# Gated DeltaNet in a two-layer hybrid block: k and q projected first, v only after the first batch's inverse has been written

## The chip, the cores and the metric

The kernel runs on one core of one Trainium2 chip. The metric is the time of one execution in microseconds (us), as the device reports it. The core's engines are TensorE (PE in the profile, its weight loads PEld), VectorE (DVE), ScalarE (ACT), GpSimd (POOL) and SyncE (SP), which here only issues DMA transfers.

## What is computed

The reference runs two layers over 256 context tokens and 512 latent tokens of width 1024. In each layer the tokens are normalised and modulated, multiplied by one input projection `w_in`, and its columns are shared out among four mixers: a bidirectional gated DeltaNet (GDN), a windowed attention (SWA), a spatial gating MLP and a bidirectional mLSTM. Their outputs are joined, projected and added to the stream; an MLP follows. The change is in the GDN alone, whose start is:

```python
def branch(q, k, v, a, b):
    qkv = jax.nn.silu(dwconv_centred(jnp.concatenate([q, k, v], axis=-1), conv_w))
    q, k, v = jnp.split(qkv, 3, axis=-1)
    ...
    seq = (l2norm(heads(q, GDN_HEADS)), l2norm(heads(k, GDN_HEADS)), heads(v, GDN_HEADS))
    return seq, (g, beta)
```

and whose scan, in chunks of 64 tokens, is:

```python
a = jnp.where(strict, jnp.einsum('nbhik,nbhjk->nbhij', kbeta, k) * decay, 0.0)
rhs = jnp.concatenate([v * beta[..., None], kbeta * jnp.exp(gcum)[..., None]], axis=-1)
sol = lax.linalg.triangular_solve(a + jnp.eye(GDN_CHUNK, dtype=jnp.float32), rhs,
                                  left_side=True, lower=True)
```

The decays come from the gates a and b and from no projection of q, k or v. The matrix `a` needs k, the attention needs q and k, and v stands in the right side only.

## The kernel before, in words

**Dense products.** The fp32 products are made of three half-exact ones: ScalarE rounds a weight tile into `whi` (two halves of K, L184), VectorE makes the rest `wlo` (L187), and the activations have been split likewise into `hhi` and `hlo`. The function `gemm` makes one block of 128 output columns of all 768 tokens with 48 matmuls named `mm`: 24 of 256 columns (context) and 24 of 512 columns (latent). `gemm_tok` makes token-major ones named `mmt`. A pool, `wset`, says which buffers the halves go into; each `wload` takes the next entry.

**GDN projections.** A loop of six blocks runs in the order k0, v0, k1, v1, q0, q1 (each of k, q and v is 256 columns, two blocks). Each block is a gemm; then ScalarE copies the result into `raw` and starts a five-tap convolution, VectorE adds four taps (one SCALAR_TENSOR_TENSOR of 128x770 each, L190), and a SiLU follows: three ScalarE passes with a VectorE TENSOR_SCALAR (L288) and a VectorE product. The blocks of k and q then go through `unit_rows`: a square, a matmul `l` that sums it by head, logarithm and exponential on ScalarE, and a last product on VectorE. Tiles `kq` hold k and q by block, tiles `vf` hold v. In layer 1 q is projected for the latent tokens alone.

**Gates.** Behind the loop, small matmuls `gc` and `glps` and short VectorE steps (`gtmp`, `kds`) make the cumulative decays.

**GDN batches.** The 12 chunks of 64 tokens are worked in six batches of two chunks for each direction. For a batch, `gdn_pre` makes the decay matrix (matmuls `rows` and `Eps`, VectorE `rhl`, `Le`, `Re`, ScalarE `E`), the products `gq` of k with k and q, and the matrix `N` (VectorE), with fp16 copies `Nh` and `Nl`; `gdn_inv` inverts in five passes, each of them matmuls `t`, VectorE `T`, matmuls `yt`, VectorE `Y`, and a VectorE transpose `Z` (the first transpose of a batch is L860, those of the passes L875), then `zt` and `nw`; `gdn_kt` makes `egps`, `kt`, and transposes v and k with `vkT`; `gdn_scan` carries the state (`rps`, `yps`, `sps`, `ops`). The driver writes: pre, inverse and kt of the first batch, pre and inverse of the second, and then the scans with pre, inverse and kt of later batches between them.

**What sets the order.** A scheduler orders the whole layer: it takes the program's order as priority and puts an instruction on its engine's list where its own estimate has it ready. Each engine then runs its list in order. So dense gemms that are written later (`sk`, `sq` and `sv` of the attention, the blocks of the spatial MLP and the mLSTM) stand among the steps of the GDN's inverse and scan.

Of the kernel before, what the change touches and what calls it, by code (L numbers as in the profile page):

```python
# [9 lines left out]
F32 = mybir.dt.float32  # L10
# [14 lines left out]
EPS = 1e-6  # L25
NEG = -1e30
GAP = NT + 2
P1 = [1, 0, 5, 4, 3, 2]
MIXK = (4, 5, 0, 1, 6, 7, 2, 3)
ALL = ((0, 256), (256, 512))  # L30
# [4 lines left out]
C_GQ, C_GK, C_GV, C_GZ, C_AB = 0, 256, 512, 768, 1024  # L35
# [107 lines left out]
def flow_kernel(ctx, tc, t, out, dbg=None, stop=None):  # L143
# [9 lines left out]
    wsp = ctx.enter_context(tc.tile_pool(name="wsp", bufs=2))  # L153
# [311 lines left out]
    wset = []  # L465
# [29 lines left out]
    def gemm(parts, acts, segs, n=128, order=None, pb=None, w2=None):  # L495

        w2 = w2 or wload(parts, order)
        outs = {bank(c0): (pb or ps)("mm") for c0, cn in segs}
        for hf, (whi, wlo) in enumerate(w2):
            for c0, cn in segs:  # L500
                o = outs[bank(c0)]
                for k in range(4):
                    ahi, alo = acts[4 * hf + k]
                    for pi, (w, a) in enumerate(((whi, ahi), (whi, alo), (wlo, ahi))):
                        mm(o[0:n, 0:cn], w[:, k, 0:n], a[:, c0:c0 + cn],
                           start=(hf == 0 and k == 0 and pi == 0), stop=(hf == 1 and k == 3 and pi == 2))
        return outs
# [92 lines left out]
    for l in range(DEPTH):  # L600
# [16 lines left out]
        gd = pa.enter_context(tc.tile_pool(name="gd", bufs=1))  # L617
# [6 lines left out]
        h = modulated(l, 0, ALL, nrm, tp)  # L624
# [4 lines left out]

        def temp(tag, w=GAP + 4):  # L630
            return tp.tile([128, GAP + 4], F32, tag=tag, name=tag, bufs=1 if tag == "tc" else 2)


        zg = temp("ta")
        o, o_k0 = gemm_pair(ahead, h, ALL, (32, 128))
        evac(zg[0:32], o, ALL, 32)
        o = ps("gatesT")
# [44 lines left out]
            else:  # L682
                stt(x[:, a0:], x[:, a0:], f, e[:, a0:], MUL, MUL)

        cols = [(C_GK, C_GQ, C_GV)[which] + 128 * j for which, j in ((0, 0), (2, 0), (0, 1), (2, 1), (1, 0), (1, 1))]
        ready = {}
        for i, (which, j) in enumerate(((0, 0), (2, 0), (0, 1), (2, 1), (1, 0), (1, 1))):
            qlat = which == 1 and last
            segs = LAT if qlat else ALL
            o = gemm(None, h, segs, w2=ready.pop(i)) if i else o_k0  # L690
            if i < 5:
                ready[i + 1] = wload([win[:, cols[i + 1]:cols[i + 1] + 128]])
            raw = temp("ta")
            G.memset(raw[:, 0:2], 0.0)
            G.memset(raw[:, 258:260], 0.0)
            G.memset(raw[:, 772:774], 0.0)
            if not qlat:
                act_(raw[:, 2:258], o[0][:, 0:256], AF.Copy)
            act_(raw[:, 260:772], o[1], AF.Copy)
            a0 = 258 if qlat else 0  # L700
            acc = vf[j] if which == 2 else kq[j][:, which]
            cw = R_CONV + {0: 2, 1: 0, 2: 4}[which] + j
            act_(acc[:, a0:], raw[:, a0:GAP], AF.Copy, scale=prm[l][:, cw:cw + 1])
            for tp_ in range(1, 5):
                stt(acc[:, a0:], raw[:, a0 + tp_:GAP + tp_], prm[l][:, cw + 6 * tp_:cw + 6 * tp_ + 1], acc[:, a0:], MUL, ADD)
            e = temp("tb")[:, 0:GAP] if i % 2 else gd.tile([128, 1024], F32, tag="at", name="e", bufs=2)[:, 0:GAP]
            sigmoid_(acc[:, a0:], e[:, a0:])
            tt(acc[:, a0:], acc[:, a0:], e[:, a0:], MUL)
            if len(unit) > 2 - 1:
                unit_rows()  # L710
            if which < 2:
                act_(e[:, a0:], acc[:, a0:], AF.Square)
                unit.append((acc, e, a0, 0.125 if which else None))
        while unit:
            unit_rows()

# [11 lines left out]
        o = ps("gc")  # L728
# [22 lines left out]
        for f in range(2):  # L751
            o = ps("glps")
# [4 lines left out]
                act_(glq[hp, :, :, f, :], o[hp, q:48:2].rearrange("p (s t h) -> p s t h", s=6, t=2), AF.Exp)  # L757


        wset[:] = [(wsp, "whi", "wlo")]  # L760
        mix = [None] * 8
        O = [xm.tile([128, NT], F32, tag="xm", name="O") for _ in range(2)]
        for x in O:
# [235 lines left out]

        gdn_pre(0)  # L1000
        gdn_inv(0)
        gdn_kt(0)
        gdn_pre(1)
        gdn_inv(1)
# [26 lines left out]
        o = gemm([win[:, C_SK:C_SK + 128]], h, ALL)  # L1031
        evac(sk, o, ALL)
        for g in range(2):
            mix[2 + g] = xm.tile([128, NT], F32, tag="xm", name="sq")
            o = gemm([win[:, C_SQ + 64 * g:C_SQ + 64 * g + 64], win[:, C_SQ + 128 + 64 * g:C_SQ + 192 + 64 * g]], h, osegs)
# [5 lines left out]
        o = gemm([win[:, C_SV:C_SV + 128]], h, ALL)  # L1041
# [11 lines left out]
        o = ps("wsT")  # L1053
# [19 lines left out]
        for p0, pn in ((0, 4), (4, 2)):  # L1073
            o = ps("svT")
# [15 lines left out]
        for j in range(2):  # L1090
            mix[4 + j] = xm.tile([128, NT], F32, tag="xm", name="uu")
            if early:
                o = gemm([win[:, C_MU + 128 * j:C_MU + 128 * j + 128]], h, osegs)
# [7 lines left out]
        for j in range(2):  # L1101
            mix[6 + j] = xm.tile([128, NT], F32, tag="xm", name="lq")
            for dst, base, sg2 in ((lk[j], C_LK, ALL), (mix[6 + j], C_LQ, osegs)):
                o = gemm([win[:, base + 128 * j:base + 128 * j + 128]], h, sg2)
# [4 lines left out]
        for j in range(2):  # L1109
            for p0 in range(opairs[0], NP, 4):  # L1110
                pn = min(4, NP - p0)
                o = ps("sg")
# [15 lines left out]
        o = gi("mb")  # L1128
# [17 lines left out]
        for p0, pn in ((0, 4), (4, 2)):  # L1146
            o = go1("aRp")
# [3 lines left out]
        o = gi("blp")  # L1151
# [50 lines left out]
        o = gi("Mt")  # L1202
# [4 lines left out]
        o = go1("Ml")  # L1207
# [344 lines left out]
        for n in range(8):  # L1552
            o = gemm([t["w_out"][l][:, 128 * n:128 * n + 128]], mh, osegs, order=MIXK, w2=w_next.pop() if w_next else None)
# [7 lines left out]
        w2 = [wload([t["mlp_w1"][l][:, 128 * f:128 * f + 128]]) for f in range(2)]  # L1561
# [3 lines left out]
        for fb in range(4):  # L1565
            hid = []
            for f in range(8):
                if fb == 0 and f < 2:
                    o = first[f]
                else:  # L1570
                    o = gemm([t["mlp_w1"][l][:, 1024 * fb + 128 * f:1024 * fb + 128 * f + 128]], h2, osegs)
# [65 lines left out]
```

## Time and profile before

| | |
|---|---|
| time, median of 3 runs | 1955.21 us (1955.19 to 1955.52) |
| the profiled execution | 1955.14 us, of which 1953.4 us span from the first to the last instruction |
| TensorE busy | 1874.8 us (96%), its weight loads 1536.4 us (79%) |
| VectorE busy | 1201.8 us (62%) |
| ScalarE busy | 757.4 us (39%) |
| mean granted TensorE clock | 0.977 of full speed |

The GDN of layer 0 lies at about 66 to 322 us of the span, that of layer 1 at about 1170 to 1405 us. Busy time of an engine is a sum over stages with different limits, so the stages are read apart, by windows; and a busy TensorE is not one at its peak, since the ends of matmuls are modelled.

### The profile page before, as it was taken

The numbers are of one execution on the slowest core, as the hardware profiler recorded it, in microseconds if no ns is written. First come the engines' busy times: TensorE is split into PE (matmuls) and PEld (weight loads), VectorE is DVE, ScalarE is ACT, GpSimd is POOL, SyncE is SP. The second block draws the span as 40 slices with busy tenths as digits, with TensorE's granted clock in tenths as the row PEclk, the third lists the DMA queues.
The fourth block names the chain that finished last, engine by engine and source line by source line (L and its number), as shares of the span: only waits on it lengthen the run. The fifth ranks groups of instructions, "written<-read, shape, count | busy, mean of one in ns | idle before, by whom it ended". The sixth has DMA issues, their size and how long they took to land.

```text
span 1953.4 us, 34015 instructions
## 1 busy us (share of the span) xinstructions
PE 1874.8 (96%) x14131; PEld 1536.4 (79%) x14131; DVE 1201.8 (62%) x2221; ACT 757.4 (39%) x1530; POOL 104.6 (5%) x169
## 2 busy tenths in 40 slices
PE   5999999999899999999999999999999999999998
PEld 3877778778777888888888878677777778888887
DVE  3978885666769557435535349798676754444443
ACT  4652343555524312313213236434255543333242
POOL 0021110000000000000000000211100000000001
PEclk8999999999799999999999999999999999999999
DMA  8321001121464345335433222210011323333332
GB/s 310 97 52 34 13 24 34 57 65 34 147 199 129 107 131 148 116 93 151 140 87 108 78 58 55 63 35 24 23 44 33 102 81 98 97 97 97 97 97 76
DMA packets 225955, 172.56 MB, mean 88 GB/s; under 512 B 19106, under 2 KB 208008, under 8 KB 225800
## 3 DMA queue, kind: packets, MB, share of 16 engines
q1 hardware_dynamic: 219424, 153.71, 26.6%
q10 hardware_dynamic: 4680, 10.64, 1.5%
q0 software_dynamic: 1696, 6.03, 0.9%
q8 instruction: 111, 1.82, 0.4%
q14 instruction: 44, 0.36, 0.1%
HBM read 163.02 MB, written 7.34 MB: 87 GB/s over the span
## 4 chain that ended last, share of the span: by engine, by line
PE 82%; DVE 9%; ACT 3%; DMA 3%; issue 1%; POOL 1%; DVEq 0%; ACTq 0%; SPq 0%; POOLq 0%
PE mm L181 64%; PE mmt L181 3%; PE num L181 1%; PE ops L181 1%; DMA wst<-w_in 1%; PE pv L181 1%; DVE wlo L187 1%; DVE Y L187 1%; PE adaps L181 1%; PE yt L181 1%; DVE kq L190 1%; PE t L181 1%; PE pT L1353 1%; DMA adw<-ada_w 1%; PE yps L181 1%
## 5 line engine op out<-in xcount | busy, mean ns | idle before, releaser
L184 ACT ACTIVATE whi<-wst 128x512 fp32r<-128x512 f32 (+1 forms) x388 | 241.9, 627 | 683.8 <-PE mm L181 628.8
L181 PE MATMUL mm<-hhi,whi 128*128 128x512 f32 (+3 forms) x1344 | 479.5, 362 | 11.7 <-ACT hhi L184 11.0
L181 PE MATMUL mm<-hlo,whi 128*128 128x512 f32 (+3 forms) x1344 | 479.3, 357 | 1.2 <-DVE hlo L190 1.1
L181 PE MATMUL mm<-hhi,wlo 128*128 128x512 f32 (+3 forms) x1344 | 476.3, 356 | 0.0
L187 DVE TENSOR_TENSOR wlo<-wst,whi 128x512 fp32r<-128x512 f32 (+1 forms) x388 | 265.7, 689 | 312.9 <-ACT whi L184 308.5
L181 PEld LDWEIGHTS mm<-hhi,whi 128*128 128x128 f32 (+1 forms) x1344 | 252.7, 189 | 55.2 <-ACT hhi L184 14.4
L181 PEld LDWEIGHTS mm<-hlo,whi 128*128 128x128 f32 (+1 forms) x1344 | 253.9, 189 | 38.0 <-DVE hlo L190 2.3
L181 PEld LDWEIGHTS mm<-hhi,wlo 128*128 128x128 f32 (+1 forms) x1344 | 253.2, 189 | 38.6 <-issue 1.5
L181 PE MATMUL mm<-fhi,whi 128*128 128x512 f32 (+1 forms) x784 | 275.9, 352 | 0.0
L181 PE MATMUL mm<-flo,whi 128*128 128x512 f32 (+1 forms) x784 | 275.8, 352 | 0.0
L181 PE MATMUL mm<-fhi,wlo 128*128 128x512 f32 (+1 forms) x784 | 274.5, 350 | 0.0
L190 DVE SCALAR_TENSOR_TENSOR x<-mm,mod,x 128x256 f32<-128x256 f32 (+1 forms) x122 | 79.6, 653 | 139.8 <-PE mm L181 139.7
L181 PEld LDWEIGHTS mm<-fhi,whi 128*128 128x128 f32 x784 | 148.3, 189 | 21.9 <-ACT r L184 0.8
L181 PEld LDWEIGHTS mm<-fhi,wlo 128*128 128x128 f32 x784 | 148.1, 189 | 19.7
L181 PEld LDWEIGHTS mm<-flo,whi 128*128 128x128 f32 x784 | 148.4, 189 | 19.1
L190 DVE SCALAR_TENSOR_TENSOR adacc<-adw,scT,adacc 128x1024 f32<-128x1024 f32 x84 | 105.9, 1282 | 28.0 <-DMA adw<-ada_w 27.9
L187 DVE TENSOR_TENSOR flo<-r,fhi 128x768 fp32r<-128x768 f32 (+1 forms) x64 | 52.6, 825 | 39.2 <-ACT fhi L184 39.1
L184 ACT ACTIVATE fhi<-r 128x768 fp32r<-128x768 f32 (+1 forms) x64 | 47.2, 740 | 65.9 <-DVE r L187 65.9
L181 PE MATMUL mm<-mlo,whi 128*128 128x512 f32 (+1 forms) x192 | 69.7, 363 | 1.3 <-DVE mlo L187 1.3
L181 PE MATMUL mm<-mhi,whi 128*128 128x512 f32 (+1 forms) x192 | 69.5, 362 | 0.4 <-ACT mhi L184 0.4
L181 PE MATMUL mm<-mhi,wlo 128*128 128x512 f32 (+1 forms) x192 | 68.8, 359 | 0.0
L184 ACT ACTIVATE r<-mm 128x256 f32<-128x256 f32 (+1 forms) x96 | 49.1, 515 | 32.2 <-PE mm L181 32.2
(406 smaller groups left out, 2712.1 us busy)
## 6 DMA issues: line engine op xcount, KB each, us to landing
wst<-mlp_w SPq DMA_DIRECT2D x128, 512.0 KB, 3.8
adw<-ada_w SPq DMA_DIRECT2D x96, 512.0 KB, 4.1
wst<-w_in SPq DMA_DIRECT2D x44, 512.0 KB, 3.7
wst<-w_out SPq DMA_DIRECT2D x64, 128.0 KB, 3.2
xd<-x ACTq DMA_DIRECT2D x8, 384.0 KB, 3.4
x<-xd POOLq DMA_DIRECT2D x8, 384.0 KB, 5.5
xs<-x ACTq DMA_DIRECT2D x4, 512.0 KB, 7.2
wst<-w_in SPq DMA_DIRECT2D x8, 256.0 KB, 3.2
```

What stands on the lines that cost most here:

```text
L181: T.matmul(o, lhsT=l, rhs=r, start=start, stop=stop)
L184: S.activation(out=o, in_=i, func=f, **kw)
L187: (eng or V).tensor_tensor(out=o, in0=a, in1=b, op=op)
L190: V.scalar_tensor_tensor(out=o, in0=a, scalar=s, in1=b, op0=op0, op1=op1)
L1353: T.transpose(o[:, 256 * i + 128 * g:256 * i + 128 * g + 128], Ps[g][:, 128 * (i0 + i):128 * (i0 + i) + 128], ident)
```

## The change

The six blocks are now projected in the order k0, k1, q0, q1, v0, v1. The body of the loop becomes a function `project`; four calls of it stand where the loop stood, and the two calls for v stand behind the code of the first batch's inverse and ahead of its `gdn_kt`, which is the first to read v. The weight buffers switch to the pool `wsp` alone one block earlier in the text (at q1 and no longer behind the gates), and the SiLU of v uses the buffer `tb` in both blocks.

```diff
+PROJ = ((0, 0), (0, 1), (1, 0), (1, 1), (2, 0), (2, 1))
...
-        cols = [(C_GK, C_GQ, C_GV)[which] + 128 * j for which, j in ((0, 0), (2, 0), (0, 1), (2, 1), (1, 0), (1, 1))]
+        cols = [(C_GK, C_GQ, C_GV)[which] + 128 * j for which, j in PROJ]
         ready = {}
-        for i, (which, j) in enumerate(((0, 0), (2, 0), (0, 1), (2, 1), (1, 0), (1, 1))):
+
+        def project(i, o):
+
+            which, j = PROJ[i]
             qlat = which == 1 and last
             segs = LAT if qlat else ALL
-            o = gemm(None, h, segs, w2=ready.pop(i)) if i else o_k0
+            o = o or gemm(None, h, segs, w2=ready.pop(i))
...
-            e = temp("tb")[:, 0:GAP] if i % 2 else gd.tile([128, 1024], F32, tag="at", name="e", bufs=2)[:, 0:GAP]
+            e = temp("tb")[:, 0:GAP] if i % 2 or i > 3 else gd.tile([128, 1024], F32, tag="at", name="e", bufs=2)[:, 0:GAP]
...
+        for i in range(4):
+            if i == 3:
+                wset[:] = [(wsp, "whi", "wlo")]
+            project(i, None if i else o_k0)
         while unit:
             unit_rows()
...
-        wset[:] = [(wsp, "whi", "wlo")]
...
         gdn_pre(0)
         gdn_inv(0)
+        for i in (4, 5):
+            project(i, None)
         gdn_kt(0)
         gdn_pre(1)
         gdn_inv(1)
```

A line lower in the file is numbered one higher in the changed kernel (L187 becomes L188, L190 becomes L191), and the inverse's transposes L860 and L875 become L868 and L883.

The first place is VectorE's list in layer 0, up to the transpose (L860) that the first matmul `t` of the first batch's inverse reads. `kq_657` is the tile of k1 and q1, and its last product is what `gq` waits for; the rows with 1148 are the second batch's. Before:

```order
L190 SCALAR_TENSOR_TENSOR rhl<-rhi,cst,rows 64x128
L190 SCALAR_TENSOR_TENSOR Le_1148<-rhi,cst,rows 64x128
L187 TENSOR_TENSOR Re<-rhl,cst 64x512
L190 SCALAR_TENSOR_TENSOR kq_657<-kq_657,tb 128x770
L187 TENSOR_TENSOR N_1174<-gq,N_1174 128x512
L187 TENSOR_TENSOR ATb_1141<-gq,E 64x8x64 x2
L187 TENSOR_TENSOR Y<-Nh,lvl_393 64x512 x2
L187 TENSOR_TENSOR wlo<-wst,whi 128x512
L187 TENSOR_TENSOR Y<-Y,i_91 128x512
L860 STREAM_TRANSPOSE Z<-Y 128x512
```

After; `vf_658` is the tile of v0, and the transpose is L868:

```order
L188 TENSOR_TENSOR wlo<-wst,whi 128x512
L191 SCALAR_TENSOR_TENSOR vf_658<-ta,prm_265,vf_658 128x770 x3
L191 SCALAR_TENSOR_TENSOR kq_657<-kq_657,tb 128x770
L191 SCALAR_TENSOR_TENSOR vf_658<-ta,prm_265,vf_658 128x770
L188 TENSOR_TENSOR wlo<-wst,whi 128x512
L289 TENSOR_SCALAR vf_658<-vf_658 128x770
L188 TENSOR_TENSOR N_1030<-gq,N_1030 128x512
L188 TENSOR_TENSOR ATb_997<-gq,E 64x8x64 x2
L188 TENSOR_TENSOR Y<-Nh,lvl_393 64x512 x2
L188 TENSOR_TENSOR Y<-Y,i_91 128x512
L868 STREAM_TRANSPOSE Z<-Y 128x512
```

Three taps of v0's convolution now stand ahead of q1's last product, and its fourth tap, a weight split and the first VectorE step of its SiLU stand between that product and `N`; the second batch's `rhl`, `Le` and `Re` have left this place, as have its two `kd`.

The second place is VectorE's list in layer 1, from the same transpose into the first passes of the inverse. Before:

```order
L860 STREAM_TRANSPOSE Z<-Y 128x512
L187 TENSOR_TENSOR kt<-kq_11971,eg 128x128
L187 TENSOR_TENSOR kt<-kq_11972,eg 128x2x64
L187 TENSOR_TENSOR kt<-kq_11972,eg 128x128
L187 TENSOR_TENSOR T_12473<-t_12464,lvl 128x512
L187 TENSOR_TENSOR kd<-vkT,kds 128x256
L187 TENSOR_TENSOR wlo<-wst,whi 128x512
L187 TENSOR_TENSOR Y<-Y,yt 128x512
L190 SCALAR_TENSOR_TENSOR rhl<-rhi,cst,rows 64x128
L875 STREAM_TRANSPOSE Z<-Y 128x512
```

After; `vf_11973` and `vf_11974` are the tiles of v0 and v1:

```order
L868 STREAM_TRANSPOSE Z<-Y 128x512
L191 SCALAR_TENSOR_TENSOR vf_11973<-ta,prm_266,vf_11973 128x770
L188 TENSOR_TENSOR T_12329<-t_12320,lvl 128x512
L191 SCALAR_TENSOR_TENSOR vf_11973<-ta,prm_266,vf_11973 128x770
L188 TENSOR_TENSOR Y<-Y,yt 128x512
L191 SCALAR_TENSOR_TENSOR vf_11973<-ta,prm_266,vf_11973 128x770
L883 STREAM_TRANSPOSE Z<-Y 128x512
L289 TENSOR_SCALAR vf_11973<-vf_11973 128x770
L188 TENSOR_TENSOR wlo<-wst,whi 128x512
L188 TENSOR_TENSOR T_12361<-t_12352,lvl 128x512
L188 TENSOR_TENSOR Y<-Y,yt 128x512
L191 SCALAR_TENSOR_TENSOR vf_11974<-ta,prm_266,vf_11974 128x770
```

Nearly all of v's VectorE work of this layer, eight taps, two TENSOR_SCALAR and two products, now stands between the steps of the first batch's inverse, one or two rows of it behind each step: seven taps and the other four from behind the first transpose to the `Z` that `zt` gives. The second and third batches' `rhl`, `Le`, `Re` and `N` and six rows of the attention's rotation have left that stretch.

The third place is TensorE's list in layer 1 just ahead of the first `t` of the inverse, whose weight load `Nh` stands last in the first piece; `gq` and `vkT` are the small matmuls of the batches. Before:

```order
L181 MATMUL egps<-rhl,sel_r 128x128 x4
L918 MATMUL vkT<-cst,vf_11973 128x128
L919 MATMUL vkT<-cst,kq_11971 128x128
L918 MATMUL vkT<-cst,vf_11974 128x128
L919 MATMUL vkT<-cst,kq_11972 128x128
L181 MATMUL mm<-hlo,whi 128x512
L181 MATMUL mm<-hhi,wlo 128x512
L181 MATMUL gq<-kq_11971 64x64 x4
L181 MATMUL gq<-kq_11972 64x64 x4
L181 MATMUL gq<-kq_11971 64x64 x4
L181 MATMUL gq<-kq_11972 64x64 x4
L181 LDWEIGHTS Nh
```

After; the run of `mm` begins behind `gq`:

```order
L182 MATMUL mm<-hhi,wlo 128x512
L182 MATMUL mm<-hhi,whi 128x512
L182 MATMUL gq<-kq_11971 64x64 x4
L182 MATMUL gq<-kq_11972 64x64 x4
L182 MATMUL gq<-kq_11971 64x64 x4
L182 MATMUL gq<-kq_11972 64x64 x4
L182 MATMUL mm<-hlo,whi 128x512
L182 MATMUL mm<-hhi,wlo 128x512
L182 MATMUL mm<-hhi,whi 128x256
```

Now 31 dense matmuls of v's gemms, the first three of them shown, stand in a row between this `gq` and `Nh`, 5.2 us at the spacing of such matmuls in the trace; before there were five dense ones with `vkT`, `egps` and the second batch's `gq` between them. From the first `t` to `nw` of that batch there are 67 dense matmuls now and 75 before. In layer 0 the 96 matmuls of v's two gemms stand between `glps` and the first `t`, where 89 stood before, of other gemms. At the far end of layer 0's GDN the dense matmuls from the last `ops` up to `sg`, the spatial MLP's mixing product, number 160 where they numbered 72; the place of `sg` in the list is the same, row 3320 of both. Each engine issues as many instructions of each kind as before, apart from neighbours that are counted as one, and SP's list, with all weight transfers, is the same row for row.

## Rows read from the trace of the kernel before

**Rows 1.** The page: the span, and busy time of each engine.
```profile
span 1953.4 us, 34015 instructions
PE 1874.8 (96%) x14131; PEld 1536.4 (79%) x14131; DVE 1201.8 (62%) x2221; ACT 757.4 (39%) x1530; POOL 104.6 (5%) x169
```

**Rows 2.** Windows: busy us of PE, PEld, DVE, ACT, POOL; clock, DMA share, GB/s.
```profile
66.00:110.00 44.00, 43.70 (x248) 37.69 (x248) 37.74 (x68) 26.42 (x42) 1.14 (x15) 1.00 0.24 61
110.00:141.00 31.00, 27.52 (x191) 20.06 (x190) 22.59 (x42) 21.38 (x41) 9.60 (x10) 0.99 0.25 65
141.00:167.00 26.00, 25.98 (x281) 19.95 (x280) 20.72 (x36) 6.24 (x11) 1.84 (x4) 0.88 0.15 42
1217.00:1243.00 26.00, 22.71 (x211) 16.74 (x210) 20.90 (x44) 18.48 (x39) 8.59 (x10) 1.00 0.30 77
1243.00:1270.00 27.00, 27.00 (x322) 19.80 (x321) 21.84 (x38) 7.62 (x15) 4.97 (x6) 1.00 0.14 41
```

**Rows 3.** Waits of PE in 110 to 310 us: total, times, longest.
```profile
PE t L181 <- DVE Z L860: 2.2, 1, 2.2
PE t L181 <- DVE Z L875: 2.2, 5, 0.6
```

**Rows 4.** Waits of PE in 1217 to 1430 us.
```profile
PE t L181 <- DVE Z L860: 1.9, 1, 1.9
PE t L181 <- DVE Z L875: 1.1, 4, 0.4
PE egps L181 <- DVE N L187: 0.8, 1, 0.8
PE gq L181 <- ACT eg L184: 0.5, 1, 0.5
```

**Rows 5.** Timeline of PE in a dense gemm: start, duration, engine, operation.
```profile
93.28 0.28 PE L181 MATMUL mm<-hhi,wlo 128*128 128x256 f32 x1
93.40 0.40 PE L181 MATMUL mm<-hhi,whi 128*128 128x512 f32 x1
93.64 0.39 PE L181 MATMUL mm<-hlo,whi 128*128 128x512 f32 x1
```

**Rows 6.** Chain of waits in layer 0: start, duration, what held it.
```profile
111.40 0.41 PE glps L181 x4
133.14 1.38 issue
134.53 0.69 DVE N L187
141.02 0.59 PE t L181 x8
...
309.18 12.73 PE mm L181 x72
```

**Rows 7.** Chain of waits in layer 1, first batch.
```profile
1234.96 0.70 DVE N L187
1240.34 0.39 PE t L181 x8
...
1264.10 0.95 PE nw L181 x32
```

**Rows 8.** Groups of DVE in 66 to 110 us: v's own operations.
```profile
L190 DVE SCALAR_TENSOR_TENSOR vf<-ta,prm,vf 128x770 f32<-128x770 f32 x8 | 8.1, 1014 | 2.4 <-ACT vf L184 2.4
L187 DVE TENSOR_TENSOR vf<-vf,tb 128x770 f32<-128x770 f32 x2 | 1.9, 954 | 0.0
L288 DVE TENSOR_SCALAR vf<-vf 128x770 f32<-128x770 f32 x2 | 1.1, 555 | 0.0
```

**Rows 9.** Timeline of DVE in the first batch, layer 0.
```profile
136.55 2.62 DVE L187 TENSOR_TENSOR Y<-Nh,lvl 64x512 f16<-64x512 f16 x2
...
160.26 0.68 DVE L187 TENSOR_TENSOR tc<-rope,tb 128x512 f32<-128x512 f32 x1
160.86 0.68 DVE L187 TENSOR_TENSOR T<-t,lvl 128x512 f16<-128x512 f32 x1
```

## Prediction

> **What bounds the kernel now.** I read the page first: TensorE is busy for 96% of the span, its weight loads for 79%, VectorE for 62% [rows 1]. So what can be won is TensorE's idle time, and only where this change touches it. The windows say where that is. While k0 to q0 are projected, TensorE has no gap to speak of: 43.70 us of 44 [rows 2]. Between the last projection and the first inverse of layer 0 it idles 31 - 27.52 = 3.5 us, in the same stretch of layer 1 26 - 22.71 = 3.3 us; in the passes of the inverse that follow it is full again, 25.98 of 26 and 27.00 of 27 [rows 2].
>
> The waits say what it waited for. In layer 0 the single longest one is the first `t`, 2.2 us for VectorE's first transpose `Z`; the later passes together cost another 2.2 us, in five places [rows 3]. In layer 1 three waits stand close together: 0.8 us of `egps`, 0.5 us of `gq`, 1.9 us of the first `t`, 3.2 us together; the passes cost 1.1 us in four places [rows 4]. These are the same event: the dense work at hand runs out before the serial steps from q1's end through `N`, `Y` and `Z` are through.
>
> The chain of waits shows the length of that. In layer 0 it is 141.02 - 111.40 = 29.6 us from `glps` to `t` [rows 6]. In layer 1 the part from `N` to `t` is 1240.34 - 1234.96 = 5.4 us [rows 7]. The last row of [rows 6] is the one that most speaks about this change: after the last scan of layer 0 there still stand 12.7 us of dense matmuls in one run. The GDN's chain is not what ends the stage there; the dense gemms are.
>
> **The change part by part.** *The earlier start.* Two gemms of v leave the path ahead of q1. A gemm is 24 matmuls 0.12 us apart (93.28 to 93.40) and 24 matmuls 0.24 us apart (93.40 to 93.64) [rows 5], 8.6 us by these two rows; two are 17 us. The decays and the inverse of each layer start by that much sooner. But the matmuls are only moved. By the order, the run behind the last `ops` of layer 0 grows from 72 matmuls to 160, so the scan ends sooner and TensorE then does what it left out. With `sg` at the same row and the same instructions ahead of it, the end of the stage moves only by what TensorE idles less or more. I take the earlier start itself at 0 us; its cover is that dense work, and if it were not there it would be the 17 us a layer of a rival below.
>
> *The first wait in layer 0.* Three terms change it. Between `glps` and `t` the dense matmuls go from 89 to 96: seven more, at 0.12 to 0.24 us some 1.6 us of cover by their widths. The second batch's `rows`, `Eps` and `vkT` leave this stretch, and take away cover that no row of mine prices; TensorE's busy 27.52 us here hold some 15 us of dense matmuls (89 by their widths), so all the small ones are 12 us, and the ones that leave are at most a sixth of these by count: 0 to 2 us, I take 1. And `N` comes later: behind q1's last product VectorE now has a tap of v0 (1.0 us), a weight split and the TENSOR_SCALAR (0.6 us) [rows 8]. Back to back an operation starts 0.08 us sooner than its duration says (0.68 us, but 0.60 us from 160.26 to 160.86 [rows 9]), which makes these three about 0.9 + 0.6 + 0.5 = 2.0 us; before there were 1.4 us of waiting in that place [rows 6]. So `N` is later by 0.6 us, and by up to 3.4 us if the three other taps, 2.8 us, also hold q1's last product back. VectorE has 31 - 22.59 = 8.4 us idle here [rows 2], therefore I take 0.6. Sum: 2.2 - 1.6 + 1 + 0.6 = 2.2 us, so no change; bounds from -1.6 (2.2 - 1.6 + 0 + 0) to +2.8 us (2 us of cover gone and 3.4 us of delay against 1.6). Whichever way, late `Z` stays what TensorE waits for.
>
> *The passes in layer 0.* v1's taps and both last products of v go between the steps: four taps (1.0 us), one TENSOR_SCALAR (0.6), two products (0.95) [rows 8], 6.5 us; six rows of the rotation, `N` and two `ATb` of the next batch leave, nine at 0.68 [rows 9], 6.1 us. `kd`, `rhl`, `Le` and `Re` come in; VectorE had 20.72 us of 26 [rows 2], so there are 5.3 us of slack for them. 0 us, bounds 0 and +2.6.
>
> *The first wait in layer 1.* From `N` on, the 5.4 us path gains one tap of v0 ahead of the first transpose, 0.9 us: 6.3 us. Against it stand 31 dense matmuls in a row, 5.2 us. That leaves 1.1 us of waiting where there were 3.2: -2.1 us. If the tap finds a gap, -3.0; if `N` is held up by a weight split too, -1.0.
>
> *The passes in layer 1.* Here nearly all of v's VectorE work lands: seven taps (0.93 us apart), two TENSOR_SCALAR, two products, 6.5 + 1.0 + 1.8 = 9.3 us [rows 8, 9]. The inverse's own fifteen steps are 15 x 0.60 = 9.0 us [rows 9], three weight splits and the short rest some 3 us: 21 us. TensorE took 1264.10 - 1240.34 = 23.8 us from the first `t` to `nw` [rows 7], nearly all of it work; it now has 67 dense matmuls there and not 75 (at 0.12 to 0.24 us a piece, and wider ones leave, 2.6 us), with `gq`, `vkT` and `egps` for `rows`, `Eps` and the rotation's matmuls. So TensorE's own work falls to about 21 us too and VectorE is level with it, with its waits behind `t`, `yt` and `zt` still to be added. Bounds 0 and +3.5 us; I take +1.2, since v's rows can fill part of those waits.
>
> *Buffers, the blocks' order in the spatial MLP, DMA.* The switch of the weight pool, the SiLU's buffer and the changed places in later blocks add no instruction, and SP's list is the same. 0 us, with +-2 us for what moves there.
>
> **The sum.** 0 + 0 - 2.1 + 1.2 = -0.9 us on the profiled 1955.14 us gives 1954.2 us. The profiled execution is 0.07 us under the median, which doesn't matter here.
>
> **A rule weighed against the trace.** In the passes of both layers VectorE's rows begin in the order of its list, and a transpose that has its data waits for a tap that stands before it; the 2.2 us of `t` [rows 3] are of that kind. The Trainium skill, "TensorE: Matmul & The Clock Gate", section "Architectural detail: the array is 16× 32×32, not 1× 128×128", says that VectorE's and ScalarE's queues are strict first-in first-out and only weight loads are pulled ahead on TensorE; the trace agrees, in that the row order of the timeline is that of the list. By that rule alone, each tap between two steps is paid in full: that is the slower rival.
>
> **The rivals.**
> - *Slower: v's taps stand in the inverse's way.* It decides from the point where VectorE's own rows between two `t` take longer than TensorE's rows there. In layer 1 that would be +3.5 us in the passes and -1.0 at the first wait; in layer 0 +2.8 at the first wait and +2.6 in the passes: +7.9 us, 1963.0 us. For it: 21 us against 21 in layer 1. Against it: VectorE's 5.3 us of slack in layer 0, and dense matmuls behind nearly every `t` and `yt`.
> - *Faster: the first waits vanish.* If v's gemms cover the path fully, 2.2 and 3.2 us go, and the low clock too, if it goes with the wait: TensorE's granted clock is 0.88 in 141 to 167 us [rows 2], right behind that wait, a part of the time at 1.2 and not 2.4 GHz, which is up to 0.12 x 26 = 3.1 us. Together -8.5 us, 1946.6 us. For it: 31 matmuls in one run in layer 1. Against it: in layer 0 the sum leaves the wait as it is.
> - *The chain sets the end.* Then both starts count, 34 us: 1921 us. Against it stands the run of 12.7 us [rows 6].
> - *It does nothing*, because the scheduler fills the same gaps with other gemms: 1955 us; it lies inside the forecast's own range.
>
> **How the numbers follow.** The forecast's own case (the waits change by little either way) has 0.58, with 1950 to 1959 us by the bounds above; the slower rival 0.18, the faster one 0.20, the chain's end 0.04. 0.2%, 3.9 us, is about what a measurement of this kernel tells from no change. Faster by more: 0.20 + 0.04 and the low end of the forecast's case, 0.05, so 0.29. Slower by more: 0.18 and 0.03, so 0.21. Within: 0.50. The range 1946 to 1962 us leaves out the chain's end (0.04), the edge of the faster rival (0.07) and of the slower one (0.09).
>
> **What would show it.** The dense run behind layer 0's last `ops` of some 28 us and `sg` within 3 us of 309.18 + 12.73 = 321.9 us [rows 6] shows the first step right; if `sg` comes 10 us sooner, the chain did set the end. TensorE's wait of the first `t` says which of the first-wait terms held: about 2 us in layer 0, 1 us in layer 1. Waits of `t` for the passes' `Z` of over 4 us in layer 1 would be the slower rival, none of them with a full clock behind the first `t` the faster one. A new wait elsewhere, such as a weight split late behind v's taps, would make the prediction wrong by a way that I have not priced.

## Result

The changed kernel is slower. Measured beside the kernel before, its median was 1972.92 us (1970.41 to 1977.92, 5 runs) against 1955.21 us, a ratio of 1.0094 (95% interval 1.0075 to 1.0113). Two later measurements of it gave 1.0045 (1.0029 to 1.0060) and 1.0060 (1.0036 to 1.0083); they are among the experiments. So the loss is clear of noise in all three, and its size is some 0.45 to 0.95%, 9 to 18 us. The prediction was 1954.2 us and no change, with a range of 1946 to 1962 us.

The page of the changed kernel, the span and the busy times (before: [rows 1]):

```profile
span 1973.8 us, 34021 instructions
PE 1883.6 (95%) x14131; PEld 1541.1 (78%) x14131; DVE 1205.7 (61%) x2221; ACT 756.5 (38%) x1530; POOL 103.7 (5%) x169
```

The busy times have grown by little, the span by 20.4 us, so the difference is waiting and slow clock. To see where, cut both profiles at two marks in each layer, the first matmul `gatesT`, which is ahead of the GDN's blocks, and the mLSTM's first `Mt`, which is behind its last scan: from the one to the other lies the GDN stage. Windows of the kernel before, layer 0 and layer 1 (length, then busy time of PE, PEld, DVE, ACT, POOL, then the granted clock):

```profile
65.63:335.09 269.46, 258.13 (x3212) 206.01 (x3211) 207.00 (x400) 116.13 (x241) 40.93 (x59) 0.99 0.14 36
1178.56:1414.40 235.84, 226.15 (x2942) 176.66 (x2942) 195.29 (x381) 106.40 (x216) 39.26 (x59) 0.99 0.15 41
```

The same windows of the changed kernel:

```profile
65.76:337.10 271.34, 257.06 (x3211) 205.86 (x3211) 208.60 (x400) 115.61 (x241) 38.80 (x59) 0.99 0.14 36
1187.26:1433.63 246.37, 228.36 (x2920) 176.50 (x2919) 195.23 (x381) 105.62 (x215) 40.23 (x59) 0.96 0.15 39
```

Layer 0's stage is 1.9 us longer. Layer 1's is 10.5 us longer, its idle time of TensorE has gone from 235.84 - 226.15 = 9.7 us to 246.37 - 228.36 = 18.0 us, and its mean clock from 0.99 to 0.96. The loss is in layer 1. What TensorE waited for there:

```profile
PE gc L182 <- DVE gtmp L188: 3.8, 1, 3.8
PE t L182 <- DVE Z L868: 3.8, 2, 2.3
PE t L182 <- DVE Z L883: 2.5, 2, 1.9
PE yt L182 <- DVE T L188: 1.9, 3, 1.1
PE Eps L182 <- DVE Re L188: 1.6, 2, 1.0
PE mm L182 <- DVE wlo L188: 1.5, 2, 1.3
```

The first row is new: `gc`, the first matmul of the decays, waits 3.8 us for `gtmp`, and no such wait stands among those of the kernel before. The waits of the passes (`t` for L883, `yt`) are 4.4 us, where the kernel before had 1.1 us [rows 4] and 0.3 us. Of the 3.8 us in the second row the first batch's first `t` waits 1.5 us and the second batch's 2.3 us. In layer 0, whose rows answer to [rows 3], less has moved; the passes' waits are 3.8 us, before 2.2 us for `Z` and 0.6 us for `T`:

```profile
PE t L182 <- DVE Z L868: 2.5, 1, 2.5
PE yt L182 <- DVE T L188: 2.4, 4, 0.8
PE t L182 <- DVE Z L883: 1.4, 4, 0.6
```

And the run of dense matmuls behind layer 0's scan did grow, with `sg` at 323.9 us (before 321.9, [rows 6]); the chain of waits:

```profile
299.92 24.00 PE mm L182 x135
323.93 2.77 PE sg L182 x48
```

**Why `gc` waits.** Windows of layer 1 in the changed kernel: from `gatesT` to `gc`, and the two stretches behind it ([rows 2] has the ones before):

```profile
1187.30:1212.50 25.20, 21.47 (x107) 17.48 (x106) 24.52 (x48) 16.66 (x29) 1.52 (x13) 0.98 0.24 64
1212.00:1239.00 27.00, 24.90 (x148) 18.87 (x149) 17.17 (x44) 15.73 (x31) 5.06 (x7) 0.82 0.16 39
1239.00:1265.00 26.00, 22.87 (x259) 17.44 (x256) 21.20 (x34) 9.74 (x17) 2.88 (x5) 0.87 0.22 57
```

From `gatesT` to `gc` VectorE is busy for 24.52 us of 25.20, so it hardly idles, and what stands last in its list comes late. The same part of the kernel before, from `gatesT` to the end of q1's gemm, has VectorE 3.3 us idle and TensorE nearly none:

```profile
1178.60:1217.30 38.70, 38.35 (x203) 32.34 (x203) 35.42 (x67) 25.61 (x41) 0.79 (x15) 1.00 0.26 68
```

In the changed kernel the last gemm of q ends at 1208.8 us, and TensorE's next row is `gc`; the timeline of TensorE (the bracket gives the idle time ahead of it, and what ended it):

```profile
1208.38 0.39 PE L182 MATMUL mm<-hhi,wlo 128*128 128x512 f32 x1
1212.54 0.62 PE L182 MATMUL gc<-gtmp,cst 128*128 128x24 f32 x2 [3.77 <-DVE gtmp L188]
```

VectorE's timeline says what stood before most of the gates' twelve short steps:

```profile
1202.94 0.17 DVE L736 TENSOR_SCALAR gtmp<-ysp 64x24 f32<-64x24 f32 x1
1203.05 3.28 DVE L191 SCALAR_TENSOR_TENSOR kq<-ta,prm,kq 128x770 f32<-128x770 f32 x4
...
1206.71 0.75 DVE L191 SCALAR_TENSOR_TENSOR kq<-ta,prm,kq 128x512 f32<-128x512 f32 x1
1208.45 0.74 DVE L191 SCALAR_TENSOR_TENSOR kq<-ta,prm,kq 128x512 f32<-128x512 f32 x1
...
1211.18 0.95 DVE L188 TENSOR_TENSOR kq<-kq,tb 128x770 f32<-128x770 f32 x1
1212.16 0.17 DVE L188 TENSOR_TENSOR gtmp<-ysp,tokp 64x8 f32<-64x8 f32 x1
```

The gates' first two steps ran at 1202.9 us; the other ten, which had their data then, too, stand in the list behind taps and SiLU steps of k1 (128x770) and q0 (128x512) and two weight splits, and ran from 1212.16 us on. Behind this wait the granted clock is 0.82 from 1212 to 1239 us, where [rows 2] had 1.00 in 1217 to 1243 us: 0.18 x 27 = 4.9 us of TensorE's full-speed time are lost there. Of VectorE the Trainium skill, "TensorE: Matmul & The Clock Gate", section "Architectural detail: the array is 16× 32×32, not 1× 128×128", says that its queue is strictly first in, first out. The trace agrees: these rows ran in the list's order, the last ones 10 us after their data were there.

**The second batch.** VectorE's first transposes of the first two batches of layer 1, before:

```profile
1239.59 0.70 DVE L860 STREAM_TRANSPOSE Z<-Y 128x512 f16<-128x512 f16 x1
1265.14 0.71 DVE L860 STREAM_TRANSPOSE Z<-Y 128x512 f16<-128x512 f16 x1
```

In the changed kernel, with the tap of v0 ahead of the first and the `t` behind the second:

```profile
1237.12 1.01 DVE L191 SCALAR_TENSOR_TENSOR vf<-ta,prm,vf 128x770 f32<-128x770 f32 x1
1238.06 0.70 DVE L868 STREAM_TRANSPOSE Z<-Y 128x512 f16<-128x512 f16 x1
...
1278.45 0.71 DVE L868 STREAM_TRANSPOSE Z<-Y 128x512 f16<-128x512 f16 x1
1279.22 0.39 PE L182 MATMUL t<-Z,Nh 128*128 128x64 f16 x8 [2.30 <-DVE Z L868]
```

The two transposes stood 25.6 us apart and now stand 40.4 us apart. VectorE's steps of the second batch, which lay among the first batch's passes, have given way to v's rows and come behind the passes, and TensorE waits 2.3 us for them. In layer 0 the distance grew from 26.1 us to 31.4 us only, and the second batch's `t` has no such wait there.

### The profile page after: what moved, and what is told of

Its sections match the earlier page's. It is cut to its first block, busy times and chain, and to the rows that moved or that the text cites. A ratio compares the mean times of both kernels' runs of the same rounds, so it can differ in the third digit from the quotient of the medians.

```text
span 1973.8 us, 34021 instructions
## 1 busy us (share of the span) xinstructions
PE 1883.6 (95%) x14131; PEld 1541.1 (78%) x14131; DVE 1205.7 (61%) x2221; ACT 756.5 (38%) x1530; POOL 103.7 (5%) x169
## 4 chain that ended last, share of the span: by engine, by line
PE 84%; DVE 8%; DMA 3%; ACT 3%; issue 1%; POOL 0%; DVEq 0%; ACTq 0%; SPq 0%; POOLq 0%
PE mm L182 65%; PE mmt L182 3%; PE num L182 1%; DVE Y L188 1%; PE ops L182 1%; DMA wst<-w_in 1%; PE pv L182 1%; PE yt L182 1%; PE adaps L182 1%; PE pT L1363 1%; PE t L182 1%; DVE wlo L188 1%; PE yps L182 1%; PE rps L182 1%; PE scl L182 1%
## 5 line engine op out<-in xcount | busy, mean ns | idle before, releaser
L182 PE MATMUL mm<-hhi,wlo 128*128 128x512 f32 (+3 forms) x1344 | 481.3, 360 | 1.7 <-DVE wlo L188 1.7
L188 DVE TENSOR_TENSOR wlo<-wst,whi 128x512 fp32r<-128x512 f32 (+1 forms) x388 | 264.8, 686 | 320.1 <-ACT whi L185 316.5
L191 DVE SCALAR_TENSOR_TENSOR x<-mm,mod,x 128x256 f32<-128x256 f32 (+1 forms) x122 | 79.7, 654 | 140.7 <-PE mm L182 140.7
L191 DVE SCALAR_TENSOR_TENSOR adacc<-adw,scT,adacc 128x1024 f32<-128x1024 f32 x84 | 105.9, 1282 | 29.3 <-DMA adw<-ada_w 29.0
L188 DVE TENSOR_TENSOR flo<-r,fhi 128x768 fp32r<-128x768 f32 (+1 forms) x64 | 52.6, 825 | 39.2 <-ACT fhi L185 39.1
L185 ACT ACTIVATE fhi<-r 128x768 fp32r<-128x768 f32 (+1 forms) x64 | 47.3, 740 | 65.6 <-DVE r L188 65.5
```

Of the source, the lines that this page charges most:

```text
L182: T.matmul(o, lhsT=l, rhs=r, start=start, stop=stop)
L185: S.activation(out=o, in_=i, func=f, **kw)
L188: (eng or V).tensor_tensor(out=o, in0=a, in1=b, op=op)
L191: V.scalar_tensor_tensor(out=o, in0=a, scalar=s, in1=b, op0=op0, op1=op1)
```

## Experiments

Each was timed in rounds beside the kernel before; ratios are those of time to the kernel before, with a 95% interval. "Stage 1" is layer 1 from `gatesT` to `Mt` as above (before 235.8 us), "stage 0" the same of layer 0 (before 269.5 us). In the three profiles of the changed kernel stage 0 is the same within 0.4 us and stage 1 within 1.2 us, so the stages tell more than the whole time, which low-clock stretches elsewhere move by several us. Each edit also lets the scheduler order the lists anew, so that a difference of some 2 us between two programs says little. Theories, as named in the expectations: G, layer 1's decays come late on VectorE; T, v's taps stand in the way of the inverse's steps; V, without v's gemms between them the VectorE work of k, q and the gates is longer than their gemms; C, low-clock stretches fall elsewhere in any changed program.

**One layer at a time.** The order of the blocks is chosen by layer:

```diff
+        late = l == 0
+        proj = PROJ if late else ((0, 0), (2, 0), (0, 1), (2, 1), (1, 0), (1, 1))
...
-        for i in (4, 5):
+        for i in (4, 5) if late else ():
             project(i, None)
```

> The new order in layer 0 alone, the old one in layer 1. The changed kernel lost 17.7 us, in its trace 2.0 us up to the end of layer 0's GDN stage, some 4 to 6 us in and behind the mLSTM's start of layer 0, and 10.5 us in layer 1's GDN stage. Theory G (layer 1's decays come late on VectorE, 3.8 us of wait and a low clock behind it): layer 0 alone costs 2 to 5 us, 1957 to 1960 us. Theory T (v's taps stand in the way of the inverse in both layers, equally): half of the loss, 1963 to 1965 us. Theory C (low-clock stretches fall elsewhere in any changed program): anything between 1953 and 1965, with more time at 1.2 GHz in the stages that the change leaves alone.

> The new order in layer 1 alone, layer 0 as before. Theory G: 10 to 13 us of the loss come back, 1965 to 1968 us, with TensorE's wait of some 3.8 us of gc for gtmp in layer 1 as in the changed kernel. Theory T: half of the loss, 1963 to 1965 us, with the wait of gc no larger a part than the waits of the passes. Theory C: 1955 to 1960 us.

Layer 0 alone gave 1.0001 (0.9989 to 1.0014), layer 1 alone (with `l == 1`) 1.0055 (1.0038 to 1.0073). The stages, first with the change in layer 0 alone, then in layer 1 alone:

```profile
65.87:337.21 271.34, 257.06 (x3212) 205.92 (x3211) 208.42 (x400) 115.54 (x241) 38.73 (x59) 0.99 0.13 36
1180.90:1415.60 234.70, 224.87 (x2943) 175.63 (x2942) 195.39 (x381) 106.20 (x216) 39.26 (x59) 0.99 0.15 42
```

```profile
64.87:334.51 269.64, 258.29 (x3211) 206.17 (x3211) 206.96 (x400) 116.06 (x241) 40.98 (x59) 0.99 0.13 36
1178.16:1423.48 245.32, 227.28 (x2920) 175.61 (x2919) 195.12 (x381) 105.53 (x215) 40.18 (x59) 0.97 0.14 40
```

Stage 0 of the first and stage 1 of the second are those of the changed kernel (271.3 and 245 us), the others those of before. So the loss is layer 1's, against the even halves that theory T expected, and the layers don't act on each other.

**The gates early.** The loop that writes the gates' twelve short steps is moved ahead of the projections:

```diff
+        tmp = gd.tile([128, 5, 6, 2, 4], F32, tag="kt", name="gtmp")
+        ga, lb, gc, gl, cb = (tmp[:, i] for i in range(5))
+        for s_, d_ in ((0, 0), (0, 1), (1, 0), (1, 1)):
...
         cols = [(C_GK, C_GQ, C_GV)[which] + 128 * j for which, j in PROJ]
```

> The changed kernel with the twelve short VectorE steps of the gates (gtmp from ysp) written ahead of the projections, so that they stand in VectorE's list as soon as ysp is made and not behind q's taps; nothing else is moved. Theory G: the wait of gc (3.8 us) goes, and the low clock behind it too (10.2 us at 1.2 GHz, worth up to 5.1 us): 1964 to 1969 us. Theory T: the wait goes but q1's own path ends as late as it did; at most 2 us come back, 1971 to 1973 us.

1.0064 (1.0048 to 1.0081). Stage 1 falls from 245 to 240.6 us; what TensorE waits for in it follows:

```profile
1182.69:1423.31 240.62, 224.51 (x2920) 173.84 (x2919) 194.53 (x381) 105.17 (x215) 41.42 (x59) 0.98 0.15 40
```

```profile
PE t L182 <- DVE Z L868: 3.0, 2, 2.9
PE t L182 <- DVE Z L883: 2.3, 4, 1.2
PE yt L182 <- DVE T L188: 1.8, 3, 0.8
```

The wait of `gc` is gone, and 4.7 us of the stage with it, half of the loss. The low clock behind `gc` is gone, too (0.99 in the 26 us from `gc` on), while that behind the first `t` stayed (0.88 over 26 us, 0.87 in the changed kernel). A part of the wait has moved: the first `t` now waits 2.9 us. The whole time doesn't show the gain: on 1955.2 us the ratio is 1967.7 us, in theory G's range, but two of the changed kernel's own three ratios are lower.

**v's taps left out**, in the changed kernel and, as a control, in the kernel before:

```diff
-            for tp_ in range(1, 5):
+            for tp_ in range(1, 1 if which == 2 else 5):
```

> The changed kernel with the four taps of v's convolution left out (16 VectorE passes of 1 us in the two layers; the output is not the reference's). Theory T (v's taps stand between the steps of the inverse): the waits of t and yt for VectorE in the first batch of layer 1 fall under 1 us and 5 to 8 us come back. Theory G (late gates alone): the wait of gc for gtmp stays near 3.8 us, and at most 2 us come back.

> The control: the kernel before with the same taps left out. There they lie under dense gemms, so by both theories the time is that of the kernel before, within 3 us. Theory C would move it by any amount, by low-clock stretches that fall elsewhere.

1.0086 (1.0062 to 1.0111) and 1.0007 (0.9993 to 1.0021). The stages of the changed kernel without v's taps:

```profile
65.92:340.08 274.16, 261.99 (x3211) 209.73 (x3211) 203.99 (x392) 115.80 (x241) 39.12 (x59) 0.98 0.13 36
1188.09:1431.34 243.25, 226.85 (x2920) 175.35 (x2919) 188.02 (x373) 105.51 (x215) 40.23 (x59) 0.97 0.15 40
```

Stage 1 is 2 us shorter than with the taps, but so is the control's (235.8 to 233.4 us). The wait of `gc` stays at 3.8 us. Stage 0 has become 2.8 us longer, although work was left out: its clock is 0.98. So leaving out the taps brings no more in the changed kernel than before, and theory T's forecast of 5 to 8 us fails. The run doesn't price the taps by themselves, though: the waits of `t` and `yt` and of `mm` for `wlo` in stage 1 go from 9.7 to 4.5 us, and a new wait of 2.9 us, of `yps` for `Y` in the scan, stands against that.

**q's taps left out**, in both kernels, with `which == 1` in the same line.

> The changed kernel with the four taps of q's convolution left out (two blocks in each layer, some 7 us of VectorE in layer 0 and 6 us in layer 1; the output is not the reference's). Theory V (with v's gemms gone from between them, the VectorE work of k, q and the gates is longer than their gemms; in layer 1 VectorE has 0.4 us of idle in the 25 us from gatesT to gc): the wait of gc goes, the first t comes 4 us or more sooner, and the stage from gatesT to Mt of layer 1, 245.3 us, falls by 4 to 9 us. Theory T (v's taps in the passes): it stays within 1.5 us.

> The control: the kernel before with q's taps left out. Theory V: there VectorE's work lies under v's gemms, too, and only q1's own taps are on the path to the first t, so the stage of layer 1, 235.8 us, falls by less than in the changed kernel, 0 to 3 us.

1.0060 (1.0040 to 1.0080) and 1.0021 (1.0003 to 1.0039). The stages of the changed kernel without q's taps:

```profile
65.83:343.36 277.53, 259.43 (x3199) 207.36 (x3199) 200.76 (x391) 115.55 (x241) 38.53 (x59) 0.96 0.13 35
1191.14:1429.17 238.03, 226.78 (x2922) 175.74 (x2922) 188.21 (x373) 106.30 (x215) 40.32 (x59) 0.97 0.15 41
```

Stage 1 goes from 245 to 238.0 us, the wait of `gc` is gone, and the first `t` comes over 7 us sooner behind `gatesT`; the control's stage goes from 235.8 to 236.5 us. The same VectorE work that is hidden in the kernel before is worth 7 us in the changed one, where it stands ahead of the decays in layer 1. That is what theory V expected, though the control is not a clean one: it has a new wait of 3.3 us, of `l` for ScalarE. The whole time doesn't show the 7 us, since stage 0 has grown to 277.5 us: TensorE idles 18.1 us in it, not 14.3 us, and its clock is 0.96.

**Both causes at once**: the gates early and no taps of v.

> The changed kernel with the gates' short VectorE steps ahead of the projections and without v's taps (the output is not the reference's). Layer 1's stage from gatesT to Mt was 245.3 us in the changed kernel, 240.6 with the gates early, 243.2 without v's taps, 235.8 before. If the two causes are apart, they add: 238 to 239 us, and 2 to 3 us stay open. If the late start of the inverse is the one cause and the taps only lengthen it, 240 us.

1.0048 (1.0033 to 1.0063), stage 1:

```profile
1180.57:1417.14 236.57, 222.05 (x2920) 172.20 (x2919) 187.67 (x373) 104.88 (x215) 40.40 (x59) 0.99 0.15 41
```

236.6 us. That is below both expectations. With the gates early the taps are worth 4 us (240.6 to 236.6), against 2.5 us in the control. Against the control without taps, 233.4 us, 3.2 us of the loss are still there, so the taps are not all of what v's place costs.

**Where v stands.** In one run the two calls for v stand behind the gates and ahead of the first batch's decays; in a second the gates' steps are early as well; in a third all six projections are in one loop, in the new order, ahead of the gates:

```diff
-        for i in range(4):
-            if i == 3:
-                wset[:] = [(wsp, "whi", "wlo")]
+        for i in range(6):
             project(i, None if i else o_k0)
```

> v's two blocks behind the gates but ahead of the first batch's decays and inverse, so later than in the one loop and earlier than in the change. Theory G: q1's path still stands ahead of the gates on VectorE's list, as in the change, so the wait of gc stays and 4 to 7 us of the loss with it: 1.003 to 1.006 of before. Theory T: v's taps come first and the inverse finds VectorE free, so the loss goes: 0.996 to 1.001.

> The gates' short steps early and v's two blocks behind the gates' code, ahead of the first batch's decays. v behind the gates alone gave 239.0 us for layer 1's stage and 1.0033. Theory V: with the gates out of the queue of q's taps and v's gemms covering q1's path: 235 to 237 us, and 0.997 to 1.001 in all. If v must stand ahead of q1's last steps on VectorE to be harmless, it stays at 239 us.

> All six projections in one loop again, in the new order k0, k1, q0, q1, v0, v1, ahead of the gates, so that v's VectorE work has priority over the inverse and is not written behind it. Theory G: the gates are not behind on the path, since v's two gemms cover them as they did before; 1953 to 1959 us. Theory T: v's taps are out of the inverse, too, the same 1953 to 1959 us, so this run tells the two together from theory C, by which the time stays above 1962 us.

They gave 1.0033 (1.0021 to 1.0045), 1.0007 (0.9988 to 1.0025) and 0.9956 (0.9941 to 0.9971). The stages of v behind the gates, then stage 1 with the gates early too, then both stages of the one loop:

```profile
64.97:334.79 269.82, 257.05 (x3212) 205.05 (x3211) 208.47 (x400) 115.72 (x241) 39.67 (x59) 0.99 0.14 36
1182.79:1421.81 239.02, 226.82 (x2926) 176.92 (x2926) 193.66 (x381) 105.72 (x215) 40.07 (x59) 0.98 0.15 41
```

```profile
1180.84:1414.47 233.63, 223.41 (x2942) 174.18 (x2942) 194.70 (x381) 106.09 (x216) 40.14 (x59) 1.00 0.15 42
```

```profile
65.07:327.33 262.26, 251.52 (x3212) 202.27 (x3211) 204.63 (x400) 116.47 (x241) 40.23 (x59) 1.00 0.14 37
1166.42:1399.62 233.20, 223.90 (x2943) 174.44 (x2943) 192.23 (x381) 106.41 (x216) 39.83 (x59) 1.00 0.15 42
```

With v behind the gates the wait of `gc` stays at 3.8 us, as theory G has it, while the passes' waits fall from 4.4 to 1.2 us and the second batch's `t` no longer waits: its transpose is 25.1 us behind the first one, as in the kernel before. The one loop is faster than both theories had it; 0.9956 is 1946.6 us on 1955.2 us. The first two of these runs, the changed kernel (its second profile) and the gates early alone, all with nothing left out, make a square for stage 1:

| stage 1, us | gates as in the change | gates early |
|---|---|---|
| v behind the inverse (the change) | 245.2 | 240.6 |
| v ahead of the decays | 239.0 | 233.6 |

The gates' place is worth 4.6 and 5.4 us, v's place behind the inverse 6.2 and 7.0 us, and the two add. Both mended, the stage is 2 us shorter than before (235.8). So theory G is right for two fifths of it, and theory T for the rest, if it is taken as all of v's blocks, with what they push back, and not as their taps alone. The one loop and its first variant below are the fastest kernels that were run: k and q first and then v, but v's gemms behind q1's gemm and ahead of the gates, so that they cover q1's own path. Stage 0 falls from 269.5 to 262.3 us and stage 1 to 233.2 us. Of the 7.2 us in stage 0, TensorE's idle time gives 0.6 us (11.3 to 10.7). The low clock behind the first wait, worth 0.12 x 26 = 3.1 us before [rows 2], is gone, too, with 1.00 through the stage; the remaining 3.5 us were not taken apart.

**Two variants of the one loop.** With the gates early as well, and with one block of v between the blocks of k (order k0, v0, k1, q0, q1, v1):

> The one loop (k0, k1, q0, q1, v0, v1 ahead of the gates), 0.9956 of the time before, with the gates' short VectorE steps written ahead of the projections. Theory V: v's gemms cover the gates there already, so nothing changes: 0.994 to 0.998. Were the gates on the path, 2 us or more would be won.

> One loop in the order k0, v0, k1, q0, q1, v1: one block of v behind q1 and one between the blocks of k. Theory V: one gemm of 8.4 us behind q1 covers a part of q1's path (some 23 us from its gemm's end to N), v0 gives VectorE time among the blocks of k: between the kernel before and the one loop, 0.995 to 1.000. Theory C: no order in this sense, 0.998 to 1.005.

0.9958 (0.9938 to 0.9978) and 0.9990 (0.9971 to 1.0009). Early gates win nothing where v's gemms cover them; stage 1 is 235.3 us, 2.1 us longer than without. With one block of v behind q1, stage 1 is 233.3 us, that of the one loop, so one block is enough in layer 1. Stage 0 is 273.1 us; TensorE idles 12.1 us in it, little more than the one loop's 10.7 us, and its clock is 0.97, so whether one block is enough in layer 0 is not shown.

**The changed kernel again**, twice:

> The changed kernel itself once more, beside the others on one chip. The two layers apart gave 1.0001 and 1.0055 of the time before. If their losses add, 1.0056, some 11 us over the kernel before; if the first measurement's 1.0094 holds, there are 7 us more that neither layer alone has, and theory C (low-clock stretches that fall elsewhere) is the one left for them.

> The changed kernel a third time: 1.0094 at first, 1.0045 then. The stages of the GDN add 1.9 and 9.5 us, and 1.3 us come behind, in both profiles, 0.6 to 0.65%; if only the low-clock stretches outside of them differ from run to run, 1.004 to 1.008, with 271.3 and 245 to 246.5 us in the two stages.

1.0045 (1.0029 to 1.0060) and 1.0060 (1.0036 to 1.0083), with stages of 271.4 and 245.2 us in one profile and 271.8 and 245.9 us in the other. So the stages' loss of 11 to 12 us is there each time. The changed kernel's first profile has some 6 us more outside of them: from layer 0's `Mt` to layer 1's `gatesT` it took 850.2 us, in the two others 844.5 and 843.2 us, before 843.5 us. About 4 us of these lie right behind stage 0, from `Mt` to the first matmul `on`, where the same work ran at a lower clock; the first profile, then the second:

```profile
337.10:361.30 24.20, 20.71 (x131) 19.56 (x131) 10.91 (x23) 7.04 (x21) 0.00 (x0) 0.73 0.09 26
```

```profile
335.20:355.40 20.20, 16.18 (x131) 15.07 (x132) 10.85 (x24) 7.04 (x21) 0.00 (x0) 0.93 0.12 31
```

## Why the prediction was wrong

**The step that failed** is the first one, *the earlier start*, as the prediction put it: "I take the earlier start itself at 0 us; its cover is that dense work". It let the chain begin sooner by the time of v's two gemms, and took it for granted that what the chain needs is ready by then. The row behind that was layer 0's: TensorE 43.70 us of 44 busy, VectorE 37.7 [rows 2]. No row of the prediction is its mate in layer 1. There q is projected for the latent tokens alone, so a gemm of q is 24 matmuls and not 48, 24 x 0.24 = 5.8 us by [rows 5], and a tap of it still takes 0.75 us where one of a full block takes 1.0. With v's gemms out of the way VectorE is the engine that sets the time from `gatesT` to `gc` (24.52 us of 25.20), and the steps that the scheduler put last are the decays'. The measured size is 3.8 us of wait and a clock of 0.82 behind it; the early gates took 4.6 to 5.4 us of the stage back, and leaving out q's taps 7 us. The second step that failed is *the passes in layer 1*, +1.2 us with a bound of 3.5, where v's place behind the inverse cost 6 to 7 us. What it priced, the first batch from `t` to `nw`, came out within its bound: 25.8 us, before 23.6 us. But it took the second batch's steps that leave those passes as relief alone, and put no term on that batch's coming 15 us later behind the first, and on what TensorE then waits.

This is also why the start in layer 1 came sooner by less than two gemms: its first `t` stands 1238.8 - 1187.3 = 51.5 us behind `gatesT`, before 1240.3 - 1178.6 = 61.7 us: 10 us sooner and not 17. TensorE's dense work went away from there in full, and VectorE's part set what was left. In layer 0 the step held: the first `t` stands 122.5 - 65.8 = 56.7 us behind `gatesT`, before 141.0 - 65.6 = 75.4 us, and no wait of `gc` came.

**The terms.**
- *The run behind the scan*: right. `sg` came 2 us later in layer 0, not 10 us sooner, after a run of dense matmuls of 24.0 us in the chain of waits, where some 28 us were forecast and 12.7 us stood before.
- *The first wait in layer 0*: 2.2 us forecast, 2.5 us measured; right. In layer 1 1.1 us forecast, 1.5 us measured; right, and from `N` to `t` it is 1238.81 - 1232.52 = 6.3 us, as forecast, but the 3.8 us of `gc` stand in front of it. The upper bound of layer 0's term was added up wrongly: 2 + 3.4 - 1.6 is 3.8 and not 2.8 us, which makes the slower rival 8.9 us, 1964.0 us. That is still below the measured 1972.92 us.
- *The passes in layer 0*: 0 forecast; the passes' waits are 1.4 us for `Z` and 2.4 us for `T` over the layer, 1 us more than before, and the stage lost 1.9 us in all, within the bounds.
- *The passes in layer 1*: +1.2 us forecast, bounds 0 and 3.5 us. Waits for `Z` and `T` came to 4.4 us where 1.4 us were (1.1 us in [rows 4] and 0.3 us of `yt`), 3 us more, over all batches, near the upper bound. The second batch's first `t` adds 2.3 us that no term held.
- *The rule of the queue*: the prediction counted layer 0's 2.2 us of `t` before as a transpose behind a tap. No tap stands there in the kernel before, only one weight split of 0.7 us. In the changed kernel the first transpose of layer 1 does start behind a tap, about 0.9 us later than its data.
- *The low clock* was a rival's price, on the side of a gain. It went the other way in layer 1: a new wait, and the clock behind it fell.

**The rivals.** The slower rival named v's taps in the inverse, 1963.0 us, with 2.5 us in layer 1 and 5.4 in layer 0. Its place was right for more than half of the loss, in layer 1 alone, though not by the taps alone, and its own sign, waits of `t` for the passes' `Z` of over 4 us in layer 1, did not come (2.5 us); the wait of `gc` no rival named, and only the last sentence of the prediction allowed for it (a new wait elsewhere). The faster rival's mechanism, first waits that vanish with the low clock behind them, is what the one loop shows in layer 0, in an order that was not the change's: the first `t` waits 0.5 us there, not 2.2, and the clock is 1.00 through the stage.

**What stays open.** Why the first measurement was 1.0094 and the two later ones 1.0045 and 1.0060: low-clock stretches outside the GDN stage differ between profiles of the same program, but the runs don't settle what moves them. How the 6 to 7 us of v's place share out is not shown by a run of its own. The traces speak for the second batch: its first transpose in layer 1 lies 39 to 41 us behind the first batch's in every program that has v behind the inverse with its taps, 29 to 30 us without v's taps, and 25 to 28 us in every program that has v elsewhere.

## What to carry to other kernels

When work is taken out from among other work, look at the second engine of that stage and in every layer whose shapes differ: dense matmuls that left were also the time in which VectorE did its part. Read the busy share of each engine in the stretch that is to become shorter; where one of them is as long as the new stretch, it is the new bound, and what the scheduler puts last on it becomes the wait. Move filler work to where the path has nothing else to hide it (here between q1's gemm and its `N`), and no further: behind that it also pushes back the steps of the next batch that had filled the gaps there.

## What the runs showed of the hardware

Work left out can make the kernel slower: without q's taps the changed kernel's stage 0 was 277.5 us and not 271.3, with 3.8 us more of idle TensorE and a mean clock of 0.96 and not 0.99; without v's taps it was 274.2 us, with 2.1 us less of idle TensorE and a clock of 0.98. What the clock after a wait costs differs between executions of one program: behind the same 3.8 us of `gc`, it was 0.82, 0.87 and 0.83 over the next 27 us in the three profiles of the changed kernel, 4.9, 3.5 and 4.6 us lost. Not every wait was followed by a low clock: layer 1's stage of the kernel before has 3.2 us of waits ahead of and at its first `t`, and its clock was 1.00 behind them [rows 2, 4].
